# Differential attention scores: f32 matmuls with zero-padded queries, or two fp32r matmuls with stacked high and low parts

## The chip, the cores and the metric

The kernel runs on one core of one Trainium2 chip. The metric is the device time of one execution in microseconds; the profile's span is a little shorter than the time of the same execution. Engines are named as in the profile: PE is TensorE, DVE VectorE, ACT ScalarE, POOL GpSimd, SP the queue that issues nearly all DMAs of this kernel.

## The reference

One layer of a hybrid encoder, for a prompt of 512 rows and a sample of 64 rows with 256 cached rows, width 1024, all in float32. Rows are normed and projected once; half of the projection goes through a gated delta recurrence with 4 heads (chunks of 64), the other half through differential attention with 4 heads. Then come a memory attention and a feed-forward block. The change concerns the scores of the differential attention:

```
q, k: 4 heads, each with two components of 64 numbers (q1|q2, k1|k2)
s = einsum('bqhcd,bkhcd->bhcqk', q, k) * 64**-0.5      # c: component
visible = k_pos < (q_pos // 64 + 1) * 64               # whole chunks of 64
p = softmax(where(visible, s, -inf))
a = p[:, :, 0] - lam * p[:, :, 1]
o = einsum('bhqk,bkhe->bqhe', a, v)                    # then a norm per head
```

Prompt rows see prompt keys up to the end of their chunk; the sample's 64 rows see 256 cached keys and their own 64.

## The kernel before

Activations lie transposed: the feature on the partitions, 576 columns for the rows (512 prompt, then 64 sample). `HALVES` cuts the columns in 256 and 320. A projection (`project`) makes one block of 128 output features: for each half it gathers in one bank `pr` (three of them) eight slices of the contraction, with weights and activations both split in a high and a low fp32r part (`wh`, `wl`; three products, the low by low one left out). Then `evac` moves the bank to SBUF. For the first half the third product stands in the second half of the bank, and `add_to` (L193) copies it on ACT and adds the other on DVE.

The order on each engine is not written by hand here: a planner gives each instruction a priority by its place in the program, and issues on each engine's queue what is ready by its own estimate of times; on the chip every queue then runs in that fixed order. Projections, which depend on little, so fill PE while the chained work of the recurrence or of a softmax waits. Weight blocks are fetched into three `raw` buffers by SP and split by ACT and DVE (L161, L162).

The recurrence comes first in the program: `gdn_prep` for five chunks (the fifth is the sample's) and `gdn_scan` for four. Its tiles have tags in the pool `small`: At0, At1, Dt0, Dt1, Y0 and Y1 with one buffer (even and odd chunks), kd, vb, X and KQ with two. The sample's scan (`gdn_scan_sample`) is a generator whose five steps stand between the heads of the attention.

For each head h, `diff_project(h)` projects queries, keys and values (three weight blocks), and `diff_head(h)` runs five query blocks of 128 rows: t = 4 first (the sample's, with the last 64 prompt rows beside it), then t = 0 to 3 with 128, 256, 384 and 512 keys. In `diff_head`, for each component c: a score matmul into bank g0 or g1 (one of each), a mask for the upper 64 rows (L1015), a maximum (L1019), an exponent on ACT (L1022). The two components are joined (L1024 to L1027), transposed into `aT`, multiplied with the values into bank gs, and squared and copied (L1042, L1043). `finish` norms the head and puts it, transposed, into `od`, and is called within the next head.

The queries of a head are kept as one f32 tile `qz[h % 2]` of 128 x 2 x 576: for c = 0 the lower 64 partitions hold zeros in place of the second component's features, for c = 1 the upper 64 partitions do. So one f32 matmul over all 128 partitions of the keys `kdT[:, h]` makes the scores of one component. `qz` shares its place with tiles that are used earlier (gains) and later.

`od` is one half of a large tile, `e3`; the memory's rows stood there before. After the heads the memory's keys and values are projected (128 rows by 512 columns at a time, `wh` and `wl` as the moving operand), with the low parts of the keys in At0, At1, Dt0 and Dt1 and those of the values in Y0, Y1 and B1; `finish` of head 3 stands within that loop, and the output projection follows.

Of the kernel before, what the change touches and what calls it, by code (L numbers as in the profile page):

```python
# [8 lines left out]
F32 = mybir.dt.float32  # L9
F32R = mybir.dt.float32r  # L10
AF = mybir.ActivationFunctionType
ALU = mybir.AluOpType
# [3 lines left out]
P = 128  # L16
D = 1024
KT = 8
SEQ = 512
DEC = 64  # L20
T = SEQ + DEC
HALVES = ((0, 256), (256, T - 256))
PAST = 256
# [14 lines left out]
def hybrid_layer_kernel(  # L38
# [9 lines left out]
    nc = tc.nc  # L48
    V, A, G = nc.vector, nc.scalar, nc.gpsimd
# [17 lines left out]
    cp = ctx.enter_context(tc.tile_pool(name="cp", bufs=1))  # L67
# [11 lines left out]
    def nm(s):  # L79
        uid[0] += 1  # L80
        return f"{s}_{uid[0]}"
# [9 lines left out]

    def small(tag, shape, bufs=None, dt=F32):
        tag = SHARED.get(tag, tag)
        bufs = 1 if tag in ("vn", "on", "S") or tag[:-1] in ("At", "Dt", "Y") else 2
        return sp.tile(shape, dt, tag=tag, name=nm(tag), bufs=bufs)

    def tiny(shape, tag="tiny", bufs=16):
# [2 lines left out]
    def bank(tag="ba"):  # L100
        return ps.tile([P, 512], F32, tag=tag, name=nm(tag), bufs=BANKS[tag])
# [4 lines left out]
    def mm(out, lhsT, rhs, start=True, stop=True, pin=False, skip_group_check=False):  # L106
        i = nc.tensor.matmul(out, lhsT, rhs, start=start, stop=stop, skip_group_check=skip_group_check)  # L107
        if pin:
            tc.keep_in_program_order(i)
# [83 lines left out]
    def add_to(dst, b, more):  # L193
        A.copy(dst, more)
        V.tensor_tensor(dst, b, dst, ALU.add)
# [75 lines left out]
    tags = [("pr", "ba"), ("pr", "ba"), ("g0", "ba"), ("pr", "ba"), ("gs", "g1")]  # L271
# [168 lines left out]
    for typ in (1, 0, 2):  # L440
# [3 lines left out]
        for h in range(H):  # L444
# [8 lines left out]
            n = SOFF + DEC  # L453
# [21 lines left out]
    with tc.issue_after(behind_keys[1]):  # L475
        ones2, triu2 = const([P, P], "ones2"), const([P, P], "triu2")
        G.memset(ones2, 0.0)
        for i in range(2):
            R = slice(i * DEC, (i + 1) * DEC)
            G.memset(ones2[R, R], 1.0)  # L480
# [13 lines left out]
    for a0, n in HALVES:  # L494
        b = bank("pr")
# [7 lines left out]
    b = bank()  # L503
# [50 lines left out]
    for j in range(3):  # L554
        b = bank()
# [347 lines left out]
    S = None  # L903
    prepared = [gdn_prep(*chunks[0])]
    for c, _, L in chunks[:4]:
# [4 lines left out]
        S = gdn_scan(c, L, prepared[c], S)  # L910
# [4 lines left out]
    S = cp.tile([P, T], F32, tag="accq", name=nm("S"))[:, :SEQ].rearrange("p (h v) -> p h v", h=H)  # L915
# [17 lines left out]
    od, kdT = e3[:, 0], e5[:, 0]  # L933
# [2 lines left out]
    cv2 = view(e3, 1, 4, 4 * P).rearrange("p (i b) n -> p i b n", i=2)  # L936
    ckT, cvv = cv2[:, 0].rearrange("p b (c n) -> p (b c) n", n=PAST), cv2[:, 1]

    qz = [cp.tile([P, 2, T], F32, tag=f"qz{i}", name=f"qz{i}") for i in range(2)]
    with tc.issue_after(behind_keys[0]), tc.issue_after(behind_keys[1]):  # L940
        for q2 in qz:
            G.memset(q2[64:, 0, :], 0.0)
            G.memset(q2[:64, 1, :], 0.0)
        G.memset(vs[64:], 0.0)

    def diff_project(h):
        hs = slice(h * P, (h + 1) * P)
        for kind, base in (("q", 2056), ("k", 2568), ("v", 3080)):
            def evac(b, a0, n, more):
                ts_ = slice(a0, a0 + n)  # L950
                if kind == "q":
                    for c in range(2):
                        R = slice(64 * c, 64 * c + 64)
                        if more is not None:
                            add_to(qz[h % 2][R, c, ts_], b[R], more[R])
                        else:
                            (A.copy if c else V.tensor_copy)(qz[h % 2][R, c, ts_], b[R])
                    return
                d = small("zr", [P, 320])[:, :n] if kind == "v" else kdT[:, h, ts_]
                if more is not None:  # L960
                    add_to(d, b, more)
                else:
                    V.tensor_copy(d, b)
                bt = bank()
                for t in range(2):
                    tr(bt[:, t * P : (t + 1) * P], d[:, t * P : (t + 1) * P])
                if a0:
                    tr(bt[:DEC, 256:384], d[:, 256:])
                src, t2 = bt[:, :256].rearrange("p (t d) -> p t d", t=2), slice(a0 // P, a0 // P + 2)
                if kind == "v":  # L970
                    A.copy(vtm[:, t2, hs], src)
                    if a0:
                        A.copy(vs[:DEC, h, :], bt[:DEC, 256:384])
                else:
                    ko = small("ko", [P, 3, P])
                    A.copy(ko[:, :2], src)
                    nc.sync.dma_start(o_dk_p[0, 0, a0 : a0 + 256, h, :].rearrange("(t p) d -> p t d", p=P), ko[:, :2])
                    if a0:
                        A.copy(ko[:DEC, 2], bt[:DEC, 256:384])
                        nc.sync.dma_start(o_dk_s[0, 0, :, h, :], ko[:DEC, 2])  # L980

            project(weights(w2, base + h * P), xs, evac)
        nc.sync.dma_start(o_dv_p[0, 0, :, h, :].rearrange("(t p) d -> p t d", p=P), vtm[:, :, hs])
        nc.sync.dma_start(o_dv_s[0, 0, :, h, :], vs[:DEC, h, :])
# [11 lines left out]
    def diff_head(h, between):  # L996


        hs = slice(h * P, (h + 1) * P)
        so, co = tiny([P, 5], "ta"), tiny([P, 5], "ta")  # L1000
        on = small("an", [P, 5, P])
        for t in (4, 0, 1, 2, 3):
            if t == 1:
                between()
            q0 = QT[t][0]
            nk = q0 + P if t < 4 else PAST + DEC
            nb = (nk + P - 1) // P
            pr = []
            mx, l = tiny([P, 2], "ta"), tiny([P, 2], "ta")
            for c in range(2):  # L1010
                b = bank(f"g{c}")
                qq = qz[h % 2][:, c, q0 : q0 + P]
                if t < 4:
                    mm(b[:, :nk], qq, kdT[:, h, :nk])
                    V.memset(b[:64, nk - 64 : nk], -1e30)  # L1015
                else:
                    mm(b[:, :PAST], qq, ckT[:, h, :])
                    mm(b[:, PAST:nk], qq, kdT[:, h, SEQ:T])
                V.tensor_reduce(mx[:, c : c + 1], b[:, :nk], AX.X, ALU.max)  # L1019
                V.tensor_scalar(mx[:, c : c + 1], mx[:, c : c + 1], -0.125, None, ALU.mult)  # L1020
                p = small(f"p{c}", [P, 512])
                A.activation(p[:, :nk], b[:, :nk], AF.Exp, bias=mx[:, c : c + 1], scale=0.125, accum_out=l[:, c : c + 1])  # L1022
                pr.append(p)
            V.reciprocal(l, l)  # L1024
            V.tensor_tensor(l[:, 1:2], l[:, 1:2], nlam, ALU.mult)
            V.tensor_scalar(pr[1][:, :nk], pr[1][:, :nk], l[:, 1:2], None, ALU.mult)
            V.scalar_tensor_tensor(pr[0][:, :nk], pr[0][:, :nk], l[:, 0:1], pr[1][:, :nk], ALU.mult, ALU.add)  # L1027
            if nk < nb * P:
                G.memset(pr[0][:, nk : nb * P], 0.0)
            bt = bank()  # L1030
            aT = small("aT", [P, 4, P])
            for kb in range(nb):
                tr(bt[:, kb * P : (kb + 1) * P], pr[0][:, kb * P : (kb + 1) * P])
            A.copy(aT[:, :nb, :], v4(bt, nb))
            po = bank("gs")[:, :P]
            for kb in range(nb):
                if t < 4:
                    vv = vtm[:, kb, hs]
                else:
                    vv = cvv[:, kb, hs] if kb < 2 else vs[:, h, :]  # L1040
                mm(po, aT[:, kb, :], vv, start=kb == 0, stop=kb == nb - 1)
            A.activation(pr[1][:, :P], po, AF.Square, accum_out=so[:, t : t + 1])  # L1042
            A.copy(on[:, t, :], po)  # L1043

        def finish():
            V.tensor_scalar(so, so, 1.0 / P, EPS, ALU.mult, ALU.add)
            rpow(co, so)
            V.tensor_tensor(on, on, co.unsqueeze(2).to_broadcast([P, 5, P]), ALU.mult)
            b, b2 = bank(), bank()
            for t in range(4):  # L1050
                tr(b[:, t * P : (t + 1) * P], on[:, t, :])
            tr(b2[:, :P], on[:, 4, :])
            for src, ts_ in ((b, slice(0, SEQ)), (b2[:, DEC:P], slice(SEQ, T))):
                A.activation(od[:, h, ts_], src, AF.Identity, scale=dn)

        return finish
# [23 lines left out]
    for w, out in ((w_mem_k, o_mk), (w_mem_v, o_mv)):  # L1080
        dst = tokens
        for f in range(2):
            fs = slice(512 * f, 512 * f + 512)
            bs = [bank("pr") for _ in range(2)]
            for kc in range(4):
                wt = split_weights(w[0, 256 * kc : 256 * kc + 256, fs], [P, 2, 512])
                for k in (2 * kc, 2 * kc + 1):
                    for t in range(2):
                        ts_ = slice(t * P, (t + 1) * P)
                        for j, (wi, x) in enumerate(((0, mh), (0, ml), (1, mh))):  # L1090
                            mm(
                                bs[t], x[:, k, ts_], wt[wi][:, k % 2, :],
                                start=(k == 0 and j == 0), stop=(k == KT - 1 and j == 2),
# [6 lines left out]
            if out is o_mk:  # L1100
                for i in range(2):
                    b = bank()
# [79 lines left out]
    for k2 in range(KT // 2):  # L1182
        b = bank()
# [6 lines left out]
    for h in range(H):  # L1190
# [15 lines left out]
        for t, (q0, _) in enumerate(QT):  # L1206
            t0, n = TT[t]
            kk, kl = (mkT, mkl) if t < 4 else (cmT, cml)
            b = bank(("gs", "g0", "g1")[t % 3])
# [9 lines left out]
            p = small("p0", [P, 512])  # L1219
# [15 lines left out]
        for i in range(2):  # L1235
            b, b2 = bank(("g0", "gs")[i]), bank(("g1", "ba")[i])
# [8 lines left out]
            j = 2 * (h % 2) + i  # L1245
# [48 lines left out]
    raws, parts = {}, {}  # L1294
# [328 lines left out]
```

## Time and profile before

| | |
|---|---|
| median of 3 runs | 987.92 us (987.21 to 988.73) |
| the profiled execution's own time | 987.2 us |
| its span | 985.5 us |
| PE busy | 968.5 us, 98% of the span |
| DVE, ACT, POOL busy | 699.7, 530.1, 58.8 us |
| granted PE clock | 0.997 of full |
| DMA traffic | 90.75 MB, mean 92 GB/s |

A row of the profile's groups reads: line, engine, operation, output tile <- input tiles, shape, count | busy us, mean ns of one | idle us of that engine before it, and what ended the idle time. All matmuls have the line of the helper `mm` (L107), all transposes that of `tr` (L113), so they are told apart by their tiles. `kdT`, `od`, `ckT` and the recurrence's arrays are parts of large tiles and appear as `u`. An f32 tile and an fp32r tile both appear as f32 in the form of a matmul. In rows in order of time the first number is the start, the second the length from the first start to the last end, both in us; merged rows end with their count.

### The profile page before, as it was taken

How to read it: one execution, taken by the hardware profiler on the slowest of the kernel's cores; microseconds unless marked ns; L12 is line 12 of the kernel's file. 1: busy time of each engine (PE TensorE's matmuls, PEld its weight loads, DVE VectorE, ACT ScalarE, POOL GpSimd, SP SyncE). 2: the span in 40 equal slices, each digit the busy share in tenths (PEclk: the TensorE clock that was granted, in tenths of full speed). 3: DMA queues.
4: the chain of work that ended last, by engine and by line, in shares of the span. 5: the costliest groups of instructions: out<-in, count | busy, mean ns of one | idle time of the engine just before them, and what ended most of it. 6: DMA issues, size and time to landing. Idle time of an engine off the chain costs nothing.

```text
span 985.5 us, 16923 instructions
## 1 busy us (share of the span) xinstructions
PE 968.5 (98%) x6403; PEld 891.2 (90%) x6403; DVE 699.7 (71%) x1570; ACT 530.1 (54%) x1194; POOL 58.8 (6%) x127
## 2 busy tenths in 40 slices
PE   9999999999999999999999999999999999999996
PEld 7989899898888878999999999999999999999996
DVE  6666787877676676666557977657867779978674
ACT  7545575344656665444445657665544445555444
POOL 3341011101000000000000000000000000000000
PEclk9999999999999999999999999999999999999998
DMA  7432340103222647333111414222222223223202
GB/s 212 129 119 65 90 138 23 43 23 103 81 68 68 203 131 227 95 94 99 44 44 58 127 54 127 86 86 86 86 87 86 86 86 86 86 86 86 65 23 96
DMA packets 121714, 90.75 MB, mean 92 GB/s; under 512 B 5564, under 2 KB 112206, under 8 KB 121122
## 3 DMA queue, kind: packets, MB, share of 16 engines
q1 hardware_dynamic: 121266, 89.03, 30.9%
q8 instruction: 50, 0.82, 0.3%
q10 hardware_dynamic: 368, 0.66, 0.2%
q14 instruction: 30, 0.25, 0.1%
HBM read 79.93 MB, written 9.75 MB: 91 GB/s over the span
## 4 chain that ended last, share of the span: by engine, by line
PE 83%; DVE 4%; issue 3%; POOL 2%; DMA 2%; ACT 2%; POOLq 0%; ACTq 0%; SPq 0%; DVEq 0%
PE pr L107 51%; PE g L107 12%; PE ba L107 10%; PE gs L107 6%; PE ba L113 3%; PE g L113 1%; POOL tg L208 1%; DMA r<-in_w_ff_dram 1%; DVE p L457 1%; DVE wl L162 0%; DMA grow<-gdram 0%; DMA raw<-in_w_ff_dram 0%; POOL X L607 0%; POOL X L608 0%; DVE on L809 0%
## 5 line engine op out<-in xcount | busy, mean ns | idle before, releaser
L107 PE MATMUL pr<-u,wh 128*128 128x320 f32 (+2 forms) x1240 | 328.7, 343 | 1.3 <-DVE p L323 1.2
L107 PEld LDWEIGHTS pr<-u,wh 128*128 128x128 f32 x1240 | 212.3, 188 | 18.0 <-DVE p L323 1.8
L107 PE MATMUL pr<-u,wl 128*128 128x256 f32 (+1 forms) x816 | 226.7, 302 | 0.0
L107 PEld LDWEIGHTS pr<-u,wl 128*128 128x128 f32 x816 | 149.9, 189 | 2.7 <-DVE wl L388 0.2
L162 DVE TENSOR_TENSOR wl<-raw,wh 128x1024 fp32r<-128x1024 f32 x65 | 79.4, 1223 | 41.3 <-ACT wh L161 41.0
L161 ACT CAST wh<-raw 128x1024 fp32r<-128x1024 f32 x65 | 68.1, 1048 | 65.7 <-PE pr L107 50.5
L107 PE MATMUL pr<-u,w2h 128*128 128x320 f32 (+1 forms) x384 | 98.5, 340 | 0.0
L1369 ACT CAST w2h<-r 128x512 fp32r<-128x512 f32 x56 | 34.7, 620 | 87.9 <-PE pr L107 85.3
L107 PE MATMUL pr<-f,w2h 128*128 128x320 f32 (+1 forms) x288 | 74.3, 340 | 0.1
L107 PEld LDWEIGHTS pr<-u,w2h 128*128 128x128 f32 x384 | 65.0, 188 | 4.5 <-ACT u L1452 0.3
L107 PE MATMUL pr<-u,w2l 128*128 128x256 f32 (+1 forms) x256 | 65.1, 295 | 0.0
L1454 DVE TENSOR_TENSOR u<-u,pr 128x256 f32<-128x256 f32 x96 | 42.3, 448 | 16.9 <-PE pr L107 16.2
L107 PE MATMUL ba<-u,wl 128*128 128x288 f32 x360 | 53.0, 296 | 0.4 <-ACT keep L1405 0.4
L107 PEld LDWEIGHTS pr<-f,w2h 128*128 128x128 f32 x288 | 48.7, 188 | 4.0 <-issue 1.1
L107 PEld LDWEIGHTS ba<-u,wl 128*128 128x128 f32 x360 | 49.2, 188 | 1.2 <-ACT keep L1405 1.1
L107 PE MATMUL pr<-f,w2l 128*128 128x256 f32 (+1 forms) x192 | 48.8, 295 | 0.0
L107 PEld LDWEIGHTS pr<-u,w2l 128*128 128x128 f32 x256 | 46.9, 188 | 1.5
L208 POOL TENSOR_TENSOR tiny<-tiny,nhalf 128x1 f32<-128x1 f32 (+4 forms) x10 | 8.7, 870 | 631.6 <-DVE tiny L1522 529.8
L1370 DVE TENSOR_TENSOR w2l<-r,w2h 128x512 fp32r<-128x512 f32 x56 | 38.5, 688 | 10.7 <-ACT w2h L1369 10.4
L107 PE MATMUL pr<-wh,u 128*128 128x512 f32 x128 | 41.4, 401 | 0.0
L1414 ACT ACTIVATE c<-c 128x288 f32<-128x288 f32 x48 | 20.6, 443 | 29.5 <-DVE c L1413 29.5
L107 PEld LDWEIGHTS pr<-f,w2l 128*128 128x128 f32 x192 | 35.2, 188 | 1.2
(514 smaller groups left out, 2025.1 us busy)
## 6 DMA issues: line engine op xcount, KB each, us to landing
raw<-in_w_ff_dram SPq DMA_DIRECT2D x36, 512.0 KB
raw<-in_w_in_dram SPq DMA_DIRECT2D x28, 512.0 KB
r<-in_w_ff_dram SPq DMA_DIRECT2D x56, 256.0 KB
raw<-in_w_mem_k_dram SPq DMA_DIRECT2D x8, 512.0 KB
raw<-in_w_mem_v_dram SPq DMA_DIRECT2D x8, 512.0 KB
raw<-in_w_out_dram SPq DMA_DIRECT2D x8, 512.0 KB
raw<-in_w_mem_q_dram SPq DMA_DIRECT2D x8, 512.0 KB
raw<-in_w_mem_o_dram SPq DMA_DIRECT2D x8, 512.0 KB
```

What stands on the lines that cost most here:

```text
L107: i = nc.tensor.matmul(out, lhsT, rhs, start=start, stop=stop, skip_group_check=skip_group_check)
L113: i = nc.tensor.transpose(out, in_, ident[:n, :n])
L161: A.copy(wh, raw)
L162: V.tensor_tensor(wl, raw, wh.bitcast(F32), ALU.subtract)
L208: G.tensor_tensor(out, in_, bc(nhalf[: in_.shape[0], 0:1], list(in_.shape)), ALU.pow)
L457: V.scalar_tensor_tensor(yv[:, :n], cb[:, i : i + n], cwt[:, m, i : i + 1], yv[:, :n], ALU.mult, ALU.add)
L1369: A.copy(wh, src)
L1370: V.tensor_tensor(wl, src, wh.bitcast(F32), ALU.subtract)
L1414: A.activation(c, c, AF.Relu)
L1454: V.tensor_tensor(am, am, b, ALU.add)
```

## The change

The queries' and keys' prompt columns are split into a high part (rounded to fp32r) and a low part (the rest). For component c, a tile `qs[h % 2][:, c]` holds the high part of its 64 query features on partitions 0 to 63 and the low part on 64 to 127; the keys are laid out so that both halves of the partitions hold the high part of that component's keys, and in another tile both hold the low part. Two fp32r matmuls, one with each key tile, then add up all four products of a component's scores.

The queries' parts are first made in full height: for heads 0 and 1 in `od` (which is not yet in use), for heads 2 and 3 in Y0 and Y1; four DMAs from SBUF to SBUF bring them into `qs`. The keys' parts are made from `kdT` in the first pair of four tiles (At0, At1 and Dt0, Dt1 for even heads; kd, vb and X, KQ for odd ones): four DMAs fill the second pair with the second component's parts, then two DMAs overwrite the second component in the first pair with the first. The sample's scores stay f32 with zero-padded queries, now from one tile `qz` of 128 x 2 x 128, which all heads share. The components are run in the order 1, 0.

```diff
-        bufs = 1 if tag in ("vn", "on", "S") or tag[:-1] in ("At", "Dt", "Y") else 2
+        bufs = 1 if tag in ("vn", "on", "S", "qz") or tag[:-1] in ("At", "Dt", "Y") else 2
...
-    qz = [cp.tile([P, 2, T], F32, tag=f"qz{i}", name=f"qz{i}") for i in range(2)]
+    qs = [cp.tile([P, 2, T], F32R, tag=f"qz{i}", name=nm("qs")) for i in range(2)]
+    qz = small("qz", [P, 2, P])
     with tc.issue_after(behind_keys[0]), tc.issue_after(behind_keys[1]):
-        for q2 in qz:
-            G.memset(q2[64:, 0, :], 0.0)
-            G.memset(q2[:64, 1, :], 0.0)
+        G.memset(qz[64:, 0, :], 0.0)
+        G.memset(qz[:64, 1, :], 0.0)
         G.memset(vs[64:], 0.0)
+    stacked = {}
 
     def diff_project(h):
         hs = slice(h * P, (h + 1) * P)
+        if h < 2:
+            qn = [od[:, 2 * h + j, :SEQ].bitcast(F32R) for j in range(2)]
+        else:
+            qn = [small(tag, [P, SEQ], dt=F32R) for tag in ("Y0", "Y1")]
+        tags = ("kd", "vb", "X", "KQ") if h % 2 else ("At0", "At1", "Dt0", "Dt1")
+        ks = [small(tag, [P, SEQ], dt=F32R) for tag in tags]
+        stacked[h] = ks[:2], ks[2:]
         for kind, base in (("q", 2056), ("k", 2568), ("v", 3080)):
             def evac(b, a0, n, more):
                 ts_ = slice(a0, a0 + n)
+                t0 = slice(a0, min(a0 + n, SEQ))
+                n0 = t0.stop - a0
+
+                def parts(dst, src):
+                    A.copy(dst[0][:, t0], src[:, :n0])
+                    V.tensor_tensor(dst[1][:, t0], src[:, :n0], dst[0][:, t0].bitcast(F32), ALU.subtract)
+
                 if kind == "q":
-                    for c in range(2):
-                        R = slice(64 * c, 64 * c + 64)
-                        if more is not None:
-                            add_to(qz[h % 2][R, c, ts_], b[R], more[R])
-                        else:
-                            (A.copy if c else V.tensor_copy)(qz[h % 2][R, c, ts_], b[R])
+                    d = b
+                    if more is not None:
+                        d = qn[1][:, ts_].bitcast(F32)
+                        add_to(d, b, more)
+                    parts(qn, d)
+                    if a0:
+                        for c in range(2):
+                            R = slice(64 * c, 64 * c + 64)
+                            A.copy(qz[R, c, :], d[R, n - P :])
+                            for j in range(2):
+                                nc.sync.dma_start(
+                                    qs[h % 2][64 * j : 64 * j + 64, c, :SEQ].bitcast(F32), qn[j][R].bitcast(F32)
+                                )
                     return
...
+                if kind == "k":
+                    parts(stacked[h][0], d)
+                    if a0:
+                        first_, second_ = ([x.bitcast(F32) for x in pair_] for pair_ in stacked[h])
+                        for j in range(2):
+                            for R in (slice(0, 64), slice(64, P)):
+                                nc.sync.dma_start(second_[j][R], first_[j][64:])
+                        for j in range(2):
+                            nc.sync.dma_start(first_[j][64:], first_[j][:64])
                 bt = bank()
...
-            pr = []
+            pr = {}
-            for c in range(2):
+            for c in (1, 0):
                 b = bank(f"g{c}")
-                qq = qz[h % 2][:, c, q0 : q0 + P]
                 if t < 4:
-                    mm(b[:, :nk], qq, kdT[:, h, :nk])
+                    for j in range(2):
+                        mm(b[:, :nk], qs[h % 2][:, c, q0 : q0 + P], stacked[h][c][j][:, :nk], start=j == 0, stop=j == 1)
                     V.memset(b[:64, nk - 64 : nk], -1e30)
                 else:
-                    mm(b[:, :PAST], qq, ckT[:, h, :])
-                    mm(b[:, PAST:nk], qq, kdT[:, h, SEQ:T])
+                    mm(b[:, :PAST], qz[:, c, :], ckT[:, h, :])
+                    mm(b[:, PAST:nk], qz[:, c, :], kdT[:, h, SEQ:T])
...
-                pr.append(p)
+                pr[c] = p
```

## The prediction

> **What bounds the kernel now.** I read the page first (busy shares, clock, chain), then a table of the stretches around the changed code, then the groups by shape, and last the order of time of single stretches.
>
> ```profile
> span 985.5 us, 16923 instructions
> PE 968.5 (98%) x6403; PEld 891.2 (90%) x6403; DVE 699.7 (71%) x1570; ACT 530.1 (54%) x1194; POOL 58.8 (6%) x127
> PEclk9999999999999999999999999999999999999998
> PE 83%; DVE 4%; issue 3%; POOL 2%; DMA 2%; ACT 2%; POOLq 0%; ACTq 0%; SPq 0%; DVEq 0%
> ```
>
> TensorE is busy 98% of the span at full clock, and 83% of the chain that ended last is its own work. The changed code (score matmuls, evacuation of the heads' queries and keys) runs between 148 and 358 us. The table by stretch shows the part with the scores and what follows it:
>
> ```profile
> core 0: us, PE busy (x) PEld busy (x) DVE busy (x) ACT busy (x) POOL busy (x), PEclk, DMA share, GB/s
> 250.00:300.00 50.00, 49.21 (x294) 41.37 (x293) 35.15 (x121) 28.14 (x95) 2.00 (x3) 1.00 0.25 71
> 300.00:350.00 50.00, 49.85 (x292) 41.08 (x291) 33.72 (x111) 31.18 (x104) 2.79 (x4) 1.00 0.40 127
> 350.00:372.00 22.00, 21.18 (x112) 16.73 (x111) 15.40 (x23) 14.49 (x28) 1.17 (x1) 1.00 0.53 168
> 372.00:442.00 70.00, 70.00 (x409) 63.84 (x408) 44.36 (x74) 32.05 (x54) 0.00 (x0) 1.00 0.45 134
> ```
>
> In the 192 us from 250 to 442 TensorE stands still for 1.8 us (0.79, 0.15, 0.82 and 0). VectorE is busy 69 of the 100 us of the heads, ScalarE 59. So here an instruction that leaves TensorE shortens the program, as long as other matmuls are at hand wherever the new order makes a head wait. A busy TensorE is not TensorE at its peak, so I take prices from the distance between starts, not from busy sums.
>
> **Term 1, the score matmuls.** For a prompt block, each head and each of the two components is one f32 matmul of 128, 256, 384 or 512 keys; the change makes it two fp32r matmuls of the same width. The profile shows what one f32 matmul is: 4 heads x 2 components are 8 matmuls of 512 keys, and the group has 16 records.
>
> ```profile
> L107 PE MATMUL g<-u,qz 128*128 128x256 f32 x32 | 9.4, 394 | 0.0
> L107 PE MATMUL g<-u,qz 128*128 128x512 f32 x16 | 8.4, 609 | 0.0
> L107 PE MATMUL g<-u,qz 128*128 128x384 f32 x16 | 7.0, 519 | 0.0
> L107 PE MATMUL g<-u,qz 128*128 128x128 f32 x16 | 3.4, 295 | 0.1
> ```
>
> So an f32 matmul is two records with two weight loads, and the change has two records with two weight loads too: the count on TensorE stays the same (64 for the prompt scores), and what falls is the price of each. (Half of the 32 records of width 256 are the sample's, which stay f32.) The prices, in order of time:
>
> ```profile
> 259.27 1.02 PE L107 MATMUL g<-u,qz 128*128 128x256 f32 x4
> 261.61 0.86 PE L107 MATMUL g<-u,qz 128*128 128x384 f32 x2
> 264.18 0.28 PE L107 MATMUL pr<-u,wl 128*128 128x256 f32 x1
> 264.30 0.40 PE L107 MATMUL pr<-u,wh 128*128 128x512 f32 x1
> 264.53 0.28 PE L107 MATMUL pr<-u,wl 128*128 128x256 f32 x1
> 265.71 1.04 PE L107 MATMUL g<-u,qz 128*128 128x512 f32 x2
> 266.58 0.38 PE L113 MATMUL ba<-ident,p 128*128 128x128 f32 x2
> 267.87 0.61 PE L107 MATMUL gs<-u,aT 128*128 128x128 f32 x4
> ```
>
> From start to start an f32 record costs: width 512, (266.58 - 265.71) / 2 = 0.435 us; width 384, 0.86 - 0.519 = 0.34; width 256, (1.02 - 0.394) / 3 = 0.209; width 128, (0.61 - 0.295) / 3 = 0.105. An fp32r record of the projection (operands from wh and wl) costs 0.23 us at width 512 (264.30 to 264.53) and 0.12 at 256 (264.18 to 264.30); between them, for 384, 0.175. Each price holds its own weight load. For width 128 no fp32r row exists. It saves at most 0.05 (half of 0.105) and at worst it costs as much as the 256 wide one (0.12) or, if narrow passes are not sped up at all, twice 0.105. I take no saving, because the weight load is the same and 0.105 may already be its pace.
>
> Saved per record: 0.435 - 0.23 = 0.205, 0.34 - 0.175 = 0.165, 0.209 - 0.12 = 0.09, and 0: together 0.46. There are 16 records of each width, so 16 x 0.46 = 7.4 us. Bounds: with 0.05 saved at width 128, 8.2 us; with 0.105 lost there, 5.7.
>
> [...]
>
> **Term 2, evacuation work on ScalarE and VectorE.** Rows for what is removed and for what the added instructions resemble:
>
> ```profile
> L194 ACT COPY qz<-pr x8: 366/367/370, 148.5 to 300.5; 64x256 f32<-64x256 f32 x8
> L195 DVE TENSOR_TENSOR qz<-pr,qz x8: 398/422/429, 149.3 to 301.0; 64x256 f32<-64x256 f32 x8
> L957 DVE COPY qz<-pr x4: 472/479/483, 159.5 to 307.6; 64x320 f32<-64x320 f32 x4
> L957 ACT COPY qz<-pr x4: 419/421/421, 161.0 to 309.1; 64x320 f32<-64x320 f32 x4
> 244.83 1.66 ACT L201 CAST u<-u 128x512 fp32r<-128x512 f32 x3
> 245.48 1.29 DVE L202 TENSOR_TENSOR u<-u,u 128x512 fp32r<-128x512 f32 x2
> ```
>
> A head's queries now take 2 x 0.367 + 0.421 = 1.16 us of ScalarE and 2 x 0.422 + 0.479 = 1.32 of VectorE. After: ScalarE makes three copies of width 256 (about 0.37 each) and two of 64 x 128 (under 0.37 each), at most 1.85; VectorE three operations of 0.42, 1.27. The keys' split adds two copies and two subtractions of 256 columns per head: 0.74 and 0.84 us at the 256-wide prices, 1.1 and 1.3 if they cost as much as the 512-wide rows (0.55 and 0.65). Over four heads that is up to 5.7 us of ScalarE (7.2 by the dearer price) and 3.2 of VectorE (5.0). In the 100 us of the heads VectorE's 69 would become 72 to 74 and ScalarE's 59 some 65 to 66: both lie beside TensorE's work, and I cost them at nothing. If that cover is gone the price is at most the few microseconds named.
>
> **Term 3, the copies between partitions and the way of the keys.** Each head gains ten DMAs of 64 rows x 2 KB on SP's queue, four for the queries and six for the keys, and the last two of the six overwrite what the first four read, so they wait until those have landed: two rounds after the split.
>
> ```profile
> 118.45 1.24 DMA gdram<-p
> 119.77 4.02 DMA grow<-gdram
> 332.82 0.37 SPq L983 DMA_DIRECT2D out_dram<-u  x1
> SPq L157 <- DVE wl L162: 47.3, 7, 18.6
> ```
>
> No such copy is in the trace. The nearest landings are 1.24 us (10 KB) and 4.02 (256 KB); a 128 KB copy should lie between, and I take 2.5. An issue is 0.37 us of SP. The whole way of a head's keys is then the split, 2 x (0.37 + 0.42) = 1.6 us, six issues, 2.2, and two landings: 6.3 us at the lower end, 8.8 as taken, 11.8 at the upper.
>
> [...]
>
> Behind a waiting copy on SP stand the next weight loads. They wait mostly for a raw buffer to come free (the last row: 47.3 us in seven waits of SP in this part), that is, they are asked for blocks ahead of use, so a few microseconds of standing do not reach TensorE. Who waits for the copies is the first prompt score of a head:
>
> ```profile
> 248.68 0.38 ACT L774 COPY X<-g 128x256 f32<-128x256 f32 x1
> 250.17 1.52 PE L107 MATMUL g<-u,qz 128*128 128x256 f32 x8
> 252.52 0.48 PE L107 MATMUL g<-u,qz 128*128 128x128 f32 x2
> 227.51 0.42 ACT L957 COPY qz<-pr 64x320 f32<-64x320 f32 x1 [0.88 <-DVE qz L957]
> 322.04 0.48 DVE L963 COPY u<-pr 128x320 f32<-128x320 f32 x1
> 334.70 0.11 DVE L1015 MEMSET g<- 64x64 f32 x1 [0.74 <-PE g L107]
> ```
>
> Head 3 is typical: its second half of keys is evacuated at 322.04, its first prompt block has its scores at 334.70. That is 12.7 us, more than the 11.8 of the upper end, so nothing waits. Head 0 is the exception. Its split keys are put into At0, At1, Dt0 and Dt1, which the recurrence's last chunk uses until the copy at 248.68 (L774). Its first prompt score, now at 252.52, can start at 249 + 8.8 = 258, 5.3 us later. What fills this on TensorE is the projections of head 2, and behind them more:
>
> ```profile
> L107 PE MATMUL pr<-wh,u 128*128 128x512 f32 x42 | 14.3, 414 | 0.0
> L107 PE MATMUL pr<-wl,u 128*128 128x512 f32 x21 | 8.8, 419 | 0.0
> ```
>
> These are the groups of the memory's key and value projection between 250 and 358 us: 63 of its 192 matmuls (by the loops) are done while the heads run, and the other 129, at 0.23 us 30 us of work, come after. Heads that end 5 us later find this work in front of them, so I cost the late start at 0.5 us, and at 5.3 if the order of the queue doesn't let it through.
>
> The single zero-padded query tile for the sample adds one more wait. Head 1's second half of queries, now evacuated at 227.51, can only be released when head 0's sample scores (250.17) have read the tile, and keeps one of the three pr banks for 24 us. Two banks still alternate, and an evacuation of 0.8 us (0.37 + 0.42) is much shorter than the 24 matmuls x 0.145 = 3.5 us of a half. (0.145 lies between the 0.12 and 0.23 above, for 320 columns.) Nothing, and at most one evacuation per half, 0.8 us x 4 = 3.2, if it is not hidden.
>
> **Sum.** 987.2 us is the profiled execution's own time (span 985.5 and 1.7 around it). 987.2 - 7.4 + 0.5 = 980.3; the median of the runs is 0.7 higher, so I forecast 981.0. The forecast's own range: gain 8.2 and nothing lost, and 1 us of the present idle time gone with it, 978.7; gain 5.7 and the waits of 3.2 left, 985.4.
>
> **Rivals.** First, slower: the copies become the wait. The order of each queue is fixed before the run from planned times; if the plan counts a landing at 1.24 us and it takes 4.02, TensorE, which runs in order, stands at the first prompt score of each head for up to 2 x 2.78 = 5.6 us. It decides from 9.4 us in all (7.4 and the 2 us of the bound), 2.35 per head. With 2.8 per head (half of the extreme) it is 11.2 lost, 987.9 - 7.4 + 11.2 = 991.7. For it: head 0 has no slack, and DMA is at 0.40 and 0.53 of its share late in the heads. Against: 12.7 us of cover at head 3, and projections to fill.
>
> Second, no difference: the softmax chain of the heads is next in line, TensorE's idle time grows by what it saves, and only the idle share changes: 987. For it: VectorE at 69% with each block's mask, maximum and exponent in series. Against: 0.9 us of idle time in the 100 us, with 30 us of unbound matmuls behind.
>
> Third, the narrow matmuls don't get cheaper: fp32r at 128 and 256 keys costs what f32 costs or more. Without the 256's 1.4 us and with 1.7 lost at 128, the gain is 4.3 and the time 984.1, still faster; if fp32r is no cheaper in this form at all, it is the second rival's 987.
>
> **How the numbers follow.** The forecast 0.65, the third rival's smaller gain 0.10, no difference 0.10, slower 0.15. A measurement of this kernel can tell 0.2%, 2 us, from no change: the bounds are 985.9 and 989.9. The forecast and nearly all of the third rival are faster, 0.74; no difference 0.10; slower 0.16. For the range I go from 977.5, 1.2 us below the forecast's own end for luck in the order, to 990.0, which takes in no difference and the mildest part of the slower case.
>
> **What would show it.** Right: the groups of the prompt scores at 512 keys with 16 records near 400 ns instead of 609, at 384 near 345; TensorE busy 7 us less; idle time between 145 and 442 us still under 7 us; head 0's first prompt score near 258. Wrong: TensorE waiting for DMA or SP at the first score of each head; idle time of 5 us or more in the heads put down to VectorE or ScalarE; records of the 128-key scores no shorter than 295 ns. The prediction would be wrong above all if PE's idle time in the heads rises by more than 5 us.

## The result, and the profile after

| | before | after |
|---|---|---|
| median of 14 runs each, on one chip | 987.60 us (986.23 to 988.73) | 985.24 us (983.49 to 987.38) |
| the profiled execution's own time | 987.2 us | 986.7 us |
| its span | 985.5 us | 985.0 us |

The ratio is 0.9977, 95% interval 0.9970 to 0.9985: faster by 2.4 us, where 6.9 were forecast (981.0 from 987.9). The sign was right, and two thirds of the gain did not come. One execution in the experiments below, of the kernel with the cached keys loaded early, took 1877.5 us and is left out of that kernel's time.

The page of the changed kernel, first the rows that answer to the first fence of the prediction:

```profile
span 985.0 us, 17029 instructions
...
PE 965.2 (98%) x6403; PEld 891.4 (90%) x6403; DVE 699.6 (71%) x1578; ACT 534.5 (54%) x1210; POOL 56.6 (6%) x125
...
PEclk9999999999999999999999999999999999999998
...
PE 77%; DVE 8%; ACT 4%; issue 3%; DMA 2%; POOL 2%; POOLq 0%; ACTq 0%; DVEq 0%; SPq 0%
```

The number of TensorE's instructions is the same, as forecast, but its busy time falls by 3.3 us and not by 7, and its share of the chain that ended last falls from 83% to 77%: other engines are waited for more. (In a second trace of each kernel, described below, busy time falls by 5.7 us, from 969.1 to 963.4, and the share from 84% to 81%.) The table by stretch shows where. The first row is of the kernel before (one stretch earlier than the prediction's rows), the others are of the changed kernel:

```profile
205.00:250.00 45.00, 43.99 (x339) 39.70 (x337) 31.46 (x91) 21.30 (x58) 3.49 (x5) 1.00 0.28 77
```

```profile
205.00:250.00 45.00, 42.00 (x324) 37.96 (x322) 32.85 (x93) 21.45 (x59) 3.52 (x5) 1.00 0.33 81
250.00:300.00 50.00, 48.37 (x297) 42.77 (x298) 32.08 (x117) 27.08 (x94) 2.00 (x3) 0.97 0.47 122
300.00:350.00 50.00, 49.68 (x302) 42.15 (x301) 35.02 (x105) 33.58 (x107) 2.69 (x4) 1.00 0.62 186
```

Two things are new, both near 250 us. TensorE stands 3.00 us between 205 and 250 where it stood 1.01. And in the next row the granted clock is 0.97 instead of 1.00, which no idle time shows. In order of time, TensorE of the changed kernel:

```profile
246.31 0.40 PE L113 MATMUL g<-ident,Dt 128*128 128x128 f32 x2
...
247.27 0.46 PE L107 MATMUL pr<-u,wh 128*128 128x320 f32 x2
250.58 0.51 PE L107 MATMUL pr<-u,wh 128*128 128x512 f32 x1 [2.85 <-DVE zr L195]
...
251.03 0.40 PE L107 MATMUL pr<-u,wh 128*128 128x512 f32 x1
251.26 0.38 PE L107 MATMUL pr<-u,wl 128*128 128x256 f32 x1
251.44 0.63 PE L107 MATMUL pr<-u,wh 128*128 128x512 f32 x1
251.87 1.91 PE L113 MATMUL ba<-ident,p 128*128 128x128 f32 x8
...
254.79 1.42 PE L107 MATMUL g<-u,qz 128*128 128x256 f32 x8
...
257.48 0.44 PE L107 MATMUL g<-Dt,qs 128*128 128x128 f32 x2
```

TensorE stands from 247.73 to 250.58, 2.85 us in one piece. The narrow stretches around it (same columns as above) show the clock:

```profile
247.70:250.60 2.90, 0.05 (x2) 0.03 (x1) 2.78 (x6) 1.48 (x3) 0.00 (x0) 1.00 0.83 194
251.30:254.70 3.40, 3.40 (x15) 3.12 (x14) 0.00 (x0) 1.17 (x2) 0.00 (x0) 0.50 0.89 195
254.70:260.00 5.30, 5.19 (x32) 4.34 (x32) 2.92 (x11) 2.21 (x8) 0.00 (x0) 1.00 0.91 237
```

From 251.3 to 254.7 TensorE runs at half clock. A record of width 512 takes 0.23 us from start to start before it (251.03 to 251.26) and 0.43 within it (251.44 to 251.87). 3.4 us at half speed are 1.7 us lost. The stand and the half clock together are 2.85 + 1.7 = 4.55 us.

Why TensorE stood is read on three other queues. VectorE of the changed kernel, then a row of its ScalarE, and then its SP queue:

```profile
247.93 0.84 DVE L868 TENSOR_TENSOR on<-vb,gs 64x256 f32<-64x256 f32 x2
248.84 1.23 DVE L162 TENSOR_TENSOR wl<-raw,wh 128x1024 fp32r<-128x1024 f32 x1
250.10 0.42 DVE L195 TENSOR_TENSOR zr<-pr,zr 128x256 f32<-128x256 f32 x1
```

```profile
256.25 0.53 ACT L975 COPY qz<-pr 64x128 f32<-64x128 f32 x2 [1.84 <-PE g L107]
```

```profile
244.88 0.46 SPq L994 DMA_DIRECT2D At<-At  x1
246.78 1.10 SPq L992 DMA_DIRECT2D Dt<-At  x2
247.92 0.59 SPq L1021 DMA_DIRECT2D p<-in_cache_diff_k_dram  x1
```

TensorE wanted to begin the queries of head 2. Of the three pr banks one still held head 1's queries (pinned until the sample scores of head 0, at 254.79, have read the shared `qz` tile; the copies at 256.25 release it), and two held the halves of head 1's values, which VectorE fetches only from 250.10 on, behind two subtractions of the sample's recurrence and a split of weights. The other work that could have stood in the hole is the transposes of the cached keys (`diff_cache`) and with them the sample scores. The second load for it (L1021) was issued only at 247.92, directly behind two copies of the high parts of head 0's keys into Dt0 (L992), and these can go only when the recurrence has done with Dt0, which its last chunk, the sample's, uses: TensorE reads it last at 246.31, and the copies follow at 246.78. All waits of SP between 245.3 and 248 (0.9, 0.5 and 0.4 us) are put down to these copies and none to the load. TensorE itself does not wait for that load. Its order is fixed before the run (the two traces of the kernel before have its matmuls from 246 to 255 us in one order, 0.37 us apart at the sample scores), and in this order the transposes stand behind the first matmuls of head 2's queries, at 251.87 and with no idle time in front; so if the late load is the cause, it works through the order that the planner made. In the kernel before nothing of that kind stood in SP's queue, and the same load went out 6.3 us earlier:

```profile
241.61 0.42 SPq L990 DMA_DIRECT2D p<-in_cache_diff_k_dram  x1
```

This reading is so far an argument.

As a clock for the whole program I use four events: the first addition of the output projection (first row of each pair below), the first and the last copy of a partial product in the feed-forward part (second row, tile `keep`; the expectations below call it a column maximum), and the span. Before, then after:

```profile
L1131 DVE TENSOR_TENSOR u<-u,pr x1: 412/412/412, 393.7 to 393.7; 128x256 f32<-128x256 f32 x1
...
L1405 ACT COPY keep<-ba x48: 379/393/402, 583.2 to 930.1; 128x288 f32<-128x288 f32 x48
```

```profile
L1162 DVE TENSOR_TENSOR u<-u,pr x2: 412/450/487, 390.6 to 393.7; 128x256 f32<-128x256 f32 x1, 128x320 f32<-128x320 f32 x1
...
L1436 ACT COPY keep<-ba x48: 378/394/407, 580.7 to 929.6; 128x288 f32<-128x288 f32 x48
```

The changed kernel is 3.1 us ahead at the output projection, 2.5 at 583 us, and 0.5 at 930, so in these two traces another 2.0 us are given back in the feed-forward part, which the change does not touch.

### The profile page after: what moved, and what is told of

The parts are those of the page before. It is cut to its first block, busy times and chain, and to the rows that moved or that the text cites. A ratio compares the mean times of both kernels' runs of the same rounds, so it can differ in the third digit from the quotient of the medians.

```text
span 985.0 us, 17029 instructions
## 1 busy us (share of the span) xinstructions
PE 965.2 (98%) x6403; PEld 891.4 (90%) x6403; DVE 699.6 (71%) x1578; ACT 534.5 (54%) x1210; POOL 56.6 (6%) x125
## 4 chain that ended last, share of the span: by engine, by line
PE 77%; DVE 8%; ACT 4%; issue 3%; DMA 2%; POOL 2%; POOLq 0%; ACTq 0%; DVEq 0%; SPq 0%
PE pr L107 47%; PE g L107 10%; PE ba L107 9%; PE gs L107 6%; PE ba L113 3%; PE g L113 1%; DMA raw<-in_w_ff_dram 1%; DVE wl L162 1%; POOL tg L208 1%; DMA r<-in_w_ff_dram 1%; ACT wh L161 1%; DVE p L457 1%; DMA raw<-in_w_mem_o_dram 1%; DVE w L1300 0%; ACT wl L1299 0%
```

## The experiments

The theory: SP's queue is in order, the new copies of head 0's keys stand in it waiting, the loads of cached keys stand behind them, and so TensorE has nothing to do at 247.7. The first rival: the pinned pr bank alone does it. The second: the copies as such (their traffic, their landings, the way of the keys) cost the gain. The third: fp32r is not as cheap as forecast.

**Free the pinned bank (e1_stage).** The last 128 query columns are first copied to another buffer, so that the bank is released at once, at the price of one more copy per head.

```diff
+                        last = small("aT", [P, 4, P])[:, 0, :]
+                        A.copy(last, d[:, n - P :])
                         for c in range(2):
                             R = slice(64 * c, 64 * c + 64)
-                            A.copy(qz[R, c, :], d[R, n - P :])
+                            A.copy(qz[R, c, :], last[R])
```

> The last 128 query columns are copied from the bank into an aT buffer first and from there into the shared sample tile, so the pr bank comes free at once; one ScalarE copy (about 0.27 us) more per head. Pinned-bank theory: TensorE's 2.85 us of standing at 247.7 go, and with them the 3.4 us at half clock (1.7 us): about 980.7 us, 4.5 below the changed kernel (985.2). Late-cache theory (the sample's scores come 4.6 us late because the load of the second half of the cached keys stands on SP's queue behind the key copies): the sample scores still come near 254.8, and TensorE has head 2's queries to do meanwhile, so part of the standing may go: 982 to 985.

Measured: 986.03 us, ratio to the kernel before 0.9990 (0.9981 to 0.9999). TensorE's waits between 145 and 260 us, in the trace of this kernel (us in total, times, longest):

```profile
PE gs L107 <- DVE u L843: 1.4, 1, 1.4
PE g L107 <- DVE Y L764: 0.6, 1, 0.6
PE gs L113 <- DVE on L809: 0.5, 2, 0.3
PE ba L113 <- DVE p L1060: 0.4, 1, 0.4
```

The stand of 2.85 us is gone and the clock stays at 1.00, so the pinned bank is needed for that stand. But the first addition of the output projection comes at 391.1, no earlier than after: waits of 1.4 and 0.6 us at other places have come in with the new order, and the time is not better. Both theories had named lower times, 980.7 and 982 to 985. The pinned bank as the sole cause falls; that the test moved the order elsewhere too limits what it says.

**Load the cached keys early (e2_cache_first, run a second time as e2b_cache_first).** The two loads are asked for before the heads; nothing else is changed.

```diff
+    ckr = [small("p0", [P, 512]), small("p1", [P, 512])]
+    for bi in range(2):
+        nc.sync.dma_start(ckr[bi], cache_diff_k[0, 0, bi * P : (bi + 1) * P].rearrange("p h d -> p (h d)"))
     def diff_cache():
-        ckr = [small("p0", [P, 512]), small("p1", [P, 512])]
...
-            nc.sync.dma_start(ckr[bi], cache_diff_k[0, 0, bi * P : (bi + 1) * P].rearrange("p h d -> p (h d)"))
```

> The two loads of the cached keys are asked for before the heads, nothing else is changed. Late-cache theory: sample scores of head 0 near 250 again, no standing of TensorE before them, clock full: 980.7 us. Pinned-bank theory: head 1's queries still hold the bank until head 0's sample scores, head 2's queries can't start before, TensorE still stands 2 to 3 us before about 250: 983 to 985.

> The same kernel as e2, for a profile of an ordinary execution. Late-cache theory: head 0's sample scores near 250, TensorE standing less than 1 us between 245 and 256 and at full clock there, the output projection's first addition near 388 (changed kernel 390.6, before 393.7); time 982 to 983.

Measured: 982.05 us (the median of four executions; 982.38 with the one of 1877.5), ratio 0.9950 (0.9937 to 0.9964), and 982.74 us, ratio 0.9952 (0.9938 to 0.9965). The rows are from the second run. TensorE around the place of the stand and at head 0's first prompt score, the two stretches, and the output projection:

```profile
248.16 0.66 PE L113 MATMUL ba<-ident,p 128*128 128x128 f32 x4
248.57 0.39 PE L107 MATMUL pr<-u,wh 128*128 128x320 f32 x1
249.49 0.66 PE L113 MATMUL ba<-ident,p 128*128 128x128 f32 x4 [0.53 <-ACT u L1027]
249.94 0.50 PE L107 MATMUL pr<-u,wh 128*128 128x512 f32 x1
...
254.12 0.44 PE L107 MATMUL g<-Dt,qs 128*128 128x128 f32 x2 [0.16 <-ACT p L1055]
```

```profile
205.00:250.00 45.00, 43.64 (x338) 39.51 (x336) 32.29 (x95) 21.62 (x60) 3.52 (x5) 1.00 0.32 82
250.00:300.00 50.00, 48.65 (x307) 42.73 (x306) 36.16 (x128) 30.91 (x108) 1.99 (x3) 1.00 0.45 118
```

```profile
L1164 DVE TENSOR_TENSOR u<-u,pr x3: 414/420/489, 387.3 to 393.2; 128x256 f32<-128x256 f32 x2, 128x320 f32<-128x320 f32 x1
...
L1438 ACT COPY keep<-ba x48: 378/392/403, 576.8 to 925.7; 128x288 f32<-128x288 f32 x48
```

The transposes of the cached keys (four, then four) now come in front of the first matmul of head 2's queries (249.94), where TensorE stood, 0.53 us of the 2.85 remain, and the clock is 1.00. The copies are all still there. The kernel is 6.4 us ahead of the kernel before at the output projection, instead of 3.1. What was expected of the second run came (982 to 983, the output projection near 388); the 980.7 expected of the first was too low. The edit shows that the place of the loads matters; as it changes the plan as well as the time of the load, it does not tell these two apart.

**The same early loads in the kernel before (e4_before_cache), a control.**

> The early loads of the cached keys put into the kernel before, nothing of the change. Late-cache theory: in the kernel before these loads were not late (issued at 241.6, sample scores at 250.2 with TensorE busy up to them), so the time stays at 987.3, within 1 us. If it falls by 2 us or more, the early loads are a gain of their own and not the repair of a harm that the change did.

Measured: 988.29 us, ratio 1.0007 (0.9998 to 1.0016). The output projection begins at 393.4, at most 0.7 us earlier than without them, and the time is 1.2 us longer, just over the 1 us that was allowed for. So the early loads are no gain of their own; they are worth 2.5 us (985.24 to 982.7) only where copies stand in front of them.

**Both remedies together (e12_both).**

> Both edits, bank released at once and cached keys asked for early. Both theories: no standing of TensorE near 248 and full clock, 980 to 981 us. If it is no better than the changed kernel (985.2), neither is the cause.

Measured: 984.35 us, ratio 0.9971 (0.9959 to 0.9982), where 980 to 981 was expected; the output projection begins at 389.0. That is 1.6 us more than the early loads alone (982.74): once the cached keys are early, freeing the bank gains nothing. Whether the extra copy or the new order costs the 1.6 us isn't told apart. If the same edit costs as much without the early loads, it hid part of what freeing the bank gave in the first experiment.

**The shared sample tile alone, in the kernel before (e3_before_shared).** The scores stay f32; the sample's queries go to one tile that all heads share, which pins the bank.

```diff
+                            A.copy(qd[R, c, :], b[R, n - P :])
...
-                    mm(b[:, :PAST], qq, ckT[:, h, :])
-                    mm(b[:, PAST:nk], qq, kdT[:, h, SEQ:T])
+                    mm(b[:, :PAST], qd[:, c, :], ckT[:, h, :])
+                    mm(b[:, PAST:nk], qd[:, c, :], kdT[:, h, SEQ:T])
```

> The kernel before with one part of the change alone: the sample's scores read one shared zero-padded tile, filled straight from the pr bank (two ScalarE copies of 64x128 more per head); prompt scores stay f32, no copies between partitions. Pinned-bank theory, by itself: TensorE stands near 248 to 250 and falls to half clock, 990 to 992 us. Late-cache theory: no SP copies, so the sample scores come near 250 as before, and the time is that of before, 987.6 (plus at most 0.5).

Measured: 988.84 us, ratio 1.0016 (1.0007 to 1.0025), and no stand near 248: TensorE's longest wait between 205 and 260 is 0.5 us. So the pinned bank alone does not make the stand. The time fits neither theory. At the output projection the kernel is only 0.4 to 0.8 us late (394.5, against 393.7 and 394.1 in the two traces of the kernel before); the rest of the 1.6 us comes in the feed-forward part, so it is not shown to be the price of the bank.

**The change without its copies (e5_no_copies).** The 40 copies between partitions are left out, the queries' parts are written straight into the query tile, and the score matmuls read the unstacked parts, so the scores are not those of the reference. The part of the edit that leaves out the copies:

```diff
-                            for j in range(2):
-                                nc.sync.dma_start(
-                                    qs[h % 2][64 * j : 64 * j + 64, c, :SEQ].bitcast(F32), qn[j][R].bitcast(F32)
-                                )
...
-                                nc.sync.dma_start(second_[j][R], first_[j][64:])
-                        for j in range(2):
-                            nc.sync.dma_start(first_[j][64:], first_[j][:64])
```

> The changed kernel with all 40 copies between partitions left out: the parts are written straight into the query tile and the first pair of key tiles, and both components' score matmuls read these, so the scores' numbers are not those of the reference; matmuls, splits and the shared sample tile stay. Late-cache theory (the copies on SP's queue hold up the cached keys): sample scores near 250, no standing near 248, 980 to 981.5. Softmax theory (time saved on TensorE comes back as short waits for VectorE and ScalarE in the heads, copies or not): 984 to 986, with waits of TensorE 4 us above those of before up to the output projection.

Measured: 982.36 us, ratio 0.9951 (0.9939 to 0.9964), 0.9 us over the expected 980 to 981.5. The same two stretches of this kernel:

```profile
205.00:250.00 45.00, 43.75 (x336) 39.48 (x335) 32.54 (x94) 21.77 (x60) 3.52 (x5) 1.00 0.24 73
250.00:300.00 50.00, 48.66 (x311) 42.92 (x310) 36.20 (x127) 29.77 (x105) 2.00 (x3) 1.00 0.25 71
```

Without any copy the DMA share between 250 and 300 us is 0.25 instead of 0.45, and the time is that of the early loads within 0.4 us (the output projection begins at 387.3 in both). So beyond what the early loads give back, the copies cost nothing that can be measured, neither by their traffic nor by their landings, and the second rival falls. That their place in SP's order is what costs follows from this run and the early loads together.

**Both kernels once more, for second traces (e6_before_again, e7_after_again).**

> The kernel before, once more, for a second trace of its feed-forward stage (first addition of the gated hidden layer to last column maximum kept: 346.9 us in the first trace, 348 to 349 in those of the changed kernels). If the changed kernels lose 1 to 2 us there by what they do, this trace has again 346.9 within 0.5. If the length of that stage differs from one execution to the next, it is off by a microsecond or more, here or in the second trace of the changed kernel.

> The changed kernel once more. PE's stop of 2.85 us near 248 and the half clock behind it come from the order on SP and should be there again within 0.5 us, if they are of the program; if they are of one execution they are gone. The feed-forward stage is 348.9 again within 0.5 if its length is of the program.

Measured: 987.09 us (ratio 1.0000, 0.9989 to 1.0012) and 986.00 us (0.9980, 0.9968 to 0.9992). TensorE in the second trace of the changed kernel, then a stretch of it, in the columns of the stretches above, and the copies kept:

```profile
250.20 0.79 PE L107 MATMUL pr<-u,wh 128*128 128x512 f32 x1 [2.85 <-DVE zr L195]
```

```profile
249.70:253.10 3.40, 2.90 (x10) 2.53 (x11) 0.82 (x2) 0.00 (x0) 0.00 (x0) 0.50 0.87 216
```

```profile
L1436 ACT COPY keep<-ba x48: 377/393/405, 579.7 to 927.8; 128x288 f32<-128x288 f32 x48
```

The stand has the same length to the hundredth: it is of the program. The half clock comes again, now from 249.7 on, while TensorE still stands, but it is not in every execution. A stretch of 3.4 us at half clock lowers the mean clock over 985 us by 0.002. Of the 14 executions of the changed kernel behind its median, four have a granted clock of 0.997, as nearly all executions of the kernel before have (0.997 or 0.998), and a median of 984.4 us; the other ten have 0.995 or 0.996 and 985.8. In this second set one of eight has 0.998 and 982.45 us, the others 0.994 to 0.996 and at least 984.91. So the half clock seems to be missing in a quarter of the executions, and these are faster by about what it costs or more; no trace of one was kept, so this is not shown in order of time.

The feed-forward part gave neither kernel's first length again within 0.5 us. Its rows in the second trace of the kernel before and in the kernel before with the early loads:

```profile
L1405 ACT COPY keep<-ba x48: 380/393/406, 583.6 to 929.9; 128x288 f32<-128x288 f32 x48
```

```profile
L1407 ACT COPY keep<-ba x48: 379/393/405, 583.2 to 931.4; 128x288 f32<-128x288 f32 x48
```

From the first copy to the last it takes 927.8 - 579.7 = 348.1 us here and 348.9 in the first trace of this kernel; in the kernel before it takes 346.9 and, in its second trace, 346.3. The traces of the other kernels have 347.5 to 348.9, and the kernel before with the early loads alone has 348.2, so it takes no fp32r scores to get the longer one. TensorE's 2,683 matmuls from the first copy to the end stand in the same order before and after; three quarters of the loss or more come in five single steps of 0.2 to 0.5 us, most of them in front of a matmul that waits for an evacuation by VectorE or ScalarE. So the changed kernel takes 1.2 to 2.6 us more there. It is more than the two traces of one kernel differ (0.6 and 0.8), but every edited kernel shows it, those with f32 scores too, and what causes it stays open; no run took it away. It is part of why the time expected for the early loads was missed.

## Why the prediction was right and wrong

**Term 1, the score matmuls, 7.4 us: right.** Summed over the 80 score records of width 128 to 512 (64 of the prompt, 16 of the sample), each counted from the end of the record before it to its own end, they take 23.2 us before and 16.0 after: 7.2 less, inside the bounds of 5.7 and 8.2. (In the kernel with the early loads, whose order differs, it is 7.7 less.) In order of time, two matmuls of head 3's scores in the changed kernel with what follows each:

```profile
349.74 0.34 PE L107 MATMUL g<-KQ,qs 128*128 128x384 f32 x1
349.91 0.63 PE L107 MATMUL pr<-wh,u 128*128 128x512 f32 x2
...
352.28 0.39 PE L107 MATMUL g<-KQ,qs 128*128 128x512 f32 x1
352.51 0.39 PE L107 MATMUL pr<-wh,u 128*128 128x512 f32 x1
```

From start to start that is 0.17 us at width 384 and 0.23 at 512, against 0.175 and 0.23 taken from the projection's rows. The 16 records of width 128 take 2.48 us after and 2.42 before by the same sum: no saving, as taken, though with the early loads they take 2.03. The third rival falls.

**Term 2, evacuation work, costed at nothing: right.** The rows of the added operations in the changed kernel are 0.37 to 0.42 us for each split and 0.26 for each copy of 64 x 128. Against the operations removed this is 5.4 us more of ScalarE and 3.0 more of VectorE by the sum over the lines, where 5.7 and 3.2 stood. (The page counts overlapping instructions once: there ScalarE's busy time rises by 4.4 and VectorE's not at all.) With the early loads 6.4 of the 7.7 us saved are there at the output projection, which leaves at most 1.3 for this work and every other loss up to there.

**Term 3, the copies: this step failed, at one sentence.** It said that behind a waiting copy on SP stand the next weight loads, and that "a few microseconds of standing do not reach TensorE". For the weights that held. But SP's queue also carries the loads of the cached keys, the second of which is asked for only just ahead of use, and the prediction did not list it, though it was in the order of time of the same queue, at 241.61. It had named the two other parts of the mishap and priced each alone: head 0's keys wait for the recurrence's tiles (forecast first prompt score 258, measured 257.5), costed at 0.5, and the pinned bank, costed at nothing. Together, with the cached keys late, they left TensorE in front of a matmul that could not start, with nothing put before it that could fill the time: 2.85 us of stand and, in the traces, 1.7 of half clock. Asking for the loads early gives back 3.3 us at the output projection (390.6 to 387.3) and 2.5 of the median. The upper price of 5.3 "if the order of the queue doesn't let it through" is near that size by luck: it prices a late first prompt score, and the stand comes before that score.

**The sum.** At the output projection 3.1 us of the 7.2 are there. The missing 4.1 are about what the stand and the half clock take, 4.55, less the 0.3 us by which the other idle time between 145 and 442 us shrank (from 4.4 to 4.1). With the early loads 6.4 are there. Of these 4.4 reach the end (987.14 to 982.74): the forecast's second error is that it let the gain pass the feed-forward part whole, where 1.2 to 2.6 us are given back by a cause left open. In the two traces of the changed kernel 0.5 and 2.1 us are left at 930 us; the median of its runs is 2.4 better.

**The rivals.** The first, the copies as a wait, had the right suspect and the wrong place: TensorE does not wait for DMA at the first score of each head, it stands once, by way of a load behind the copies, and its 4.55 us stay under the 9.4 from which that rival decides. The second, the softmax chain, would have lost the gain through the heads; the early loads keep 6.4 us through the same heads, so it falls as the whole account.

**What was to show it.** Head 0's first prompt score near 258 was seen, at 257.48, but by luck: with the early loads, and every copy still in place, it starts at 254.12, so the way of the keys is shorter than the sum that gave 258, and the stand made up the difference. The wait in front of it there ends with ScalarE's exponent (L1055), not with a copy. The groups at 512 and 384 keys have a mean of 433 and 374 ns, not 400 and 345: shorter than the 609 and 519 before, though these means are not prices: the record of width 512 at 352.28 is 0.39 us long, and the next one starts 0.23 us after it. Those at 128 keys have 290 against 295, next to the sign that spoke for the third rival; as no saving was counted there, it does not touch the sum. The limit of 7 us of idle time between 145 and 442 us was just kept (6.99 by the stretches), and the idle time of the heads did not rise by 5. TensorE's busy time did not fall by 7 us (3.3 and 5.7). Both limits were blind here: half clock counts as busy time (3.40 of the 3.40 us from 251.3 on, at a clock of 0.50), and they were set too wide to find a loss of 2.85 us.

## What to carry to other kernels

Before a DMA that can wait is put on an in-order queue, list everything that the queue carries in that stretch, not only the stream that dominates it: here the wait reached a single load that is asked for just ahead of use (issued at 247.92 instead of 241.61). An order made by a planner can hide a late step only with work whose own inputs are there by the plan, so for each hole ask which instructions could fill it and what they wait for. This kernel, with TensorE at 98%, lost twice near one place, by a stand of 2.85 us and, by the granted clock in most executions, by a stretch of half clock that came with it, and the cheap remedy, two loads asked for early, gave back 2.5 us (982.7 against 985.2) without touching the change itself.

## What the hardware showed

Both traces of the changed kernel have a stand of 2.85 us and a stretch of 3.4 us at a granted clock of 0.50. The half clock began 0.7 us after TensorE had resumed in the one (251.3 against 250.58) and 0.5 us before it did in the other (249.7 against 250.20). By the mean granted clock of the executions (0.994 to 0.996, where nearly all executions of the kernel before have 0.997 or 0.998) it seems to be in 17 of the changed kernel's 22 executions, not in all. The stretches between 145 and 442 us of the first traces of both kernels and of the traces with the bank freed, the cached keys early, both remedies and no copies have a clock of 1.00 everywhere else; the longest other stand known from them is 1.4 us (the bank freed). So here half clock came with the stand of 2.85 us and with no other. What sets its beginning and its length, and how long a stand must be, is not shown.
